# The MLP of a hybrid transformer block: residual parked in the output rows, five tiles for split weights, splits made three items ahead

## The chip, the cores and the metric

The kernel runs on one core of one Trainium2 chip. The metric is the device time of one execution in microseconds (us). A core has a matrix engine (TensorE, in the profile PE, with its weight loads shown apart as PEld), a vector engine (DVE), a scalar engine for activations (ACT), GpSimd (POOL) and SyncE (SP), which here only starts transfers. Transfers (DMAs) can be started from SP, ACT or POOL.

## What is computed

One layer of a sequence model on 256 tokens of width 2048, in float32. Three mixers (two kinds of attention and an RWKV-7 recurrence) read one normed projection and are mixed through gates and an output projection. The part that matters here comes after that:

```
x = x + rms_norm(mix, norm_mix_post)              # the residual: x1 in the kernel
hdn = square(relu(rms_norm(x, norm_mlp_pre) @ w_mlp_up))     # 2048 -> 8192
x = x + rms_norm(hdn @ w_mlp_down, norm_mlp_post)            # 8192 -> 2048, the output
```

The residual x1 is used three times: as input of the up projection, in a per-token mean of squares that corrects the last norm for the norm ahead of the MLP (which the kernel leaves out of the up projection), and as the summand of the output.

## The kernel before

**Split weights.** Each float32 weight tile of 128x1024 is loaded into a tile `raw` (L160-165; `raw2` for most weights of the down projection, L1326-1333). ACT rounds it to a high part (L173, tile `whi`), DVE subtracts to get the low part (L175, `wlo`), and TensorE multiplies with both. `wsplit` (L170) does this; `home[0]` may name other tiles for the result, otherwise it takes them from a ring of three `whi` and three `wlo`. Loads are started by SP, in the order of the program; a load waits until the tile that it overwrites is free.

**Residual.** x is loaded into two tiles `x1` of 128x2048 (one for each half of the tokens, 8 KB of each partition's memory, L1159), from a pool that lives to the end. `add_mixed` (L1170) adds the normed mixer output in place, in chunks of 512 columns; TensorE transposes the result (`turn`, L1192), and ACT and DVE turn that into the 16 packed tiles `upk2`. The engines' order is written out by hand up to L1279, for POOL too from L1238 on; behind it, a scheduler orders ACT, DVE, PE, POOL and the queues by their place in the program and by what is ready.

**The MLP's work list.** The up projection gives 64 column blocks of 128; a block is two items (halves of the contraction), each of 8 products of width 512 with the high part and 8 of width 256 with the low part (`up` L1370, `gemm` L187). The second half of a block ends with a product of its own line, L197. Then `hidden` (L1348) evacuates the PSUM bank: ACT copies half of it (L1351), DVE adds the other half (L1352), ACT does relu (L1353) and square (L1357) into a tile `pk`. In blocks 2 to 9 it also squares one chunk of x1 on ACT, summing it (L1361), and after eight of them DVE makes the per-token correction `eps4` (L1363-1368). The down projection of the first 14 of 16 row groups uses a Strassen-like scheme: 28 rounds `d`, each of seven items `F1` to `F7` of six products (L1434-1436), whose weights are sums of quarter tiles. The sums are made by DVE (L1411) and by accumulating transfers that POOL starts (L1414). Three or four up items stand between the seven items of a round: three in the eight rounds of the tuple `THREE`, four in the others. Three of four PSUM tiles `gps` hold F3, F7 and F1; the fourth serves the up items.

`drive` (L1301) walks over this list. For each item it first makes the split weights of the item itself and of the next AHEAD = 1 (L1309: the `prep` of `up` or `down`), then issues the products, and behind them the postponed work of the item before (`posts`: evacuations, and `forms`, which makes the combinations of the hidden activations; `sums`: the additions of the Strassen products).

**Memory.** Ahead of the MLP the pool `op` holds gains and weight tiles `kw`; it is closed at L1477, and in its room the pool `p3` is opened for the down projection (`fm`, `sfm`, `raw2`).

**Last stage** (L1563-1590). The last two row groups go through plain products with tokens on the output side (`tok`, L208), four groups of 512 columns with four weight tiles each. After each step `tick` takes one function from the list `hooks`, which holds three empty ones and then the remaining `sums`. For each group DVE adds the sums (L1578) and ACT squares (L1579). The second last group computes the norm's constant with `eps4` (L1584), the last one the factor (`rstd_of`, with a power on POOL, L1152), multiplies, adds x1 (L1588) and writes the output in ten transfers (L1589).

Of the kernel before, what the change touches and what calls it, by code (L numbers as in the profile page):

```python
# [19 lines left out]
D = 2048  # L20
KT = 16
AHEAD = 1
SHARE = 0.88
HALF = 1024
EPS = 1e-6
# [27 lines left out]
def hybrid_block(ctx, tc, xt, x, gains, params, consts, lora, gup, wst, out):  # L53
    nc = tc.nc
    V, A, G, PE = nc.vector, nc.scalar, nc.gpsimd, nc.tensor

    cpool = ctx.enter_context(tc.tile_pool(name="cpool", bufs=1))
# [8 lines left out]
    def nm(s):  # L66
        uid[0] += 1
        return f"{s}_{uid[0]}"
# [45 lines left out]
    each, hooks = [], []  # L114
# [43 lines left out]
    rawdma = [None]  # L158
# [8 lines left out]
    home = [None]  # L167
# [114 lines left out]
    def g1(w=T):  # L282
        return rp.tile([128, T], F32, tag="g1", name=nm("g1"), bufs=21)
# [83 lines left out]
    w = {(u, 0): [wpool.tile([128, HALF], F32R, tag=t, name=nm(t), bufs=3) for t in ("whi", "wlo")] for u in range(3)}  # L367
# [666 lines left out]
    for br in ("sb", "fox"):  # L1034
        for s in ("q", "k"):
# [3 lines left out]
            for h in range(4):  # L1039
                ps = unit(upk)  # L1040
                t = g1()
# [114 lines left out]
    for f in now:  # L1156
        f()
    loads = []
    x1 = [p2.tile([128, D], F32, tag="x1", name=nm("x1"), bufs=2) for _ in range(2)]  # L1159
    for c in range(0, D, 512):  # L1160
        for tt in range(2):
            loads.append(lambda tt=tt, c=c: nc.sync.dma_start(out=x1[tt][:, c:c + 512],
                                                              in_=x[tt * 128:tt * 128 + 128, c:c + 512]))
# [3 lines left out]
    def junk():  # L1167
        return p2.tile([128, 512], F32, tag="junk", name=nm("junk"), bufs=2)

    def add_mixed(tt, c, w):  # L1170
        V.scalar_tensor_tensor(x1[tt][:, c:c + w], mg[tt][:, c:c + w], r2[tt], x1[tt][:, c:c + w], ALU.mult, ALU.add)

# [90 lines left out]
    for b in range(4):  # L1263
        add_mixed(1, 512 * b, 512)
        turn(1, b)
# [14 lines left out]
    ss3 = cpool.tile([128, 2, 4], F32, name="ss3")  # L1280
# [18 lines left out]
    work, posts, sums, hl = [], [], [], {}  # L1299

    def drive():  # L1301


        while work:
            prep, run, quota = work.pop(0)
            if prep is None:
                run(None)
                continue
            for w in [(prep, run, quota)] + [w for w in work if w[0]][:AHEAD]:  # L1309
                if w not in hl:  # L1310
# [30 lines left out]
    eps4, sum4 = [], []  # L1341
    ss4 = cpool.tile([128, 2, 4], F32, name="ss4")
    ys = []
    hid, fmh, fml = {}, {}, {}

    squares = [(tt, c) for c in range(4) for tt in range(2)]

    def hidden(j, ps):  # L1348

        b, t = tmp(), tmp()  # L1350
        A.activation(b, ps[:, T:2 * T], AF.Copy)  # L1351
        V.tensor_tensor(t, ps[:, 0:T], b, ALU.add)  # L1352
        A.activation(t, t, AF.Relu)  # L1353
        if j % 2 == 0:
            hid[j // 2] = pk().bitcast(F32).rearrange("p (s t) -> p s t", s=4)
        h = hid[j // 2]
        last = A.activation(h[:, 0:4:3] if j % 2 == 0 else h[:, 1:3], t.rearrange("p (s t) -> p s t", s=2), AF.Square)  # L1357
        if j >= 2 and squares:
            tt, c = squares.pop(0)
            with tc.issue_after(last.ins):  # L1360
                A.activation(junk(), x1[tt][:, 512 * c:512 * c + 512], AF.Square, accum_out=ss3[:, tt, c:c + 1])  # L1361
        if j in (10, 11):
            e = cpool.tile([128, 2], F32, name=nm("eps4"))  # L1363
            V.tensor_reduce(e[:, 0:1], ss3[:, j % 2, :], AX.X, ALU.add)
            V.tensor_scalar(e[:, 0:1], e[:, 0:1], 1.0 / D, EPS, ALU.mult, ALU.add)
            V.tensor_tensor(e[:, 1:2], e[:, 0:1], e[:, 0:1], ALU.mult)
            V.tensor_scalar(e[:, 1:2], e[:, 1:2], EPS, None, ALU.mult)
            eps4.append(e[:, 1:2])

    def up(j):  # L1370

# [104 lines left out]

    po.close()  # L1477
    p3 = ctx.enter_context(tc.tile_pool(name="p3", bufs=1))

    def fm():  # L1480
        return p3.tile([128, 7, 128], F32R, tag="fm", name=nm("fm"), bufs=16)
# [25 lines left out]
    for j in range(2):  # L1507
        hidden(j, gp[j])
# [27 lines left out]
    last, count, free = [], 0, 0  # L1536
    first = [sum(SIZES[:q]) for q in range(len(SIZES) + 1)]
# [3 lines left out]
    for q in range(len(SIZES)):  # L1541
        for sb in range(2):
            for d, F in enumerate(down(q, sb)):
# [10 lines left out]
                last, count, free = [F[4]], count + 1, sb  # L1554
# [3 lines left out]
    while made[0] < 32:  # L1558
        work.extend(form())
    drive()  # L1560
    hooks.extend([lambda: None] * 3 + sums)

    hp = [hp[k] for k in range(4 * LAST, 64)]  # L1563
    g4, loads = gain(1, [pk() for _ in range(4)])
    side.extend(loads)

    def spare(n):

        if n < wst.shape[0] - 3:
            return None  # L1570
        return [p3.tile([128, HALF], F32, tag="raw2", name=nm("kw"), bufs=6).bitcast(F32R) for _ in range(2)]

    home[0] = spare
    for g in range(4):
        gs = slice(512 * g, 512 * g + 512)
        for tt, ps in enumerate(tok(hp, 4 if g == 3 else 1)):
            yv = ys[tt][:, gs]
            V.tensor_tensor(yv, yv, ps, ALU.add)  # L1578
            A.activation(junk(), yv, AF.Square, accum_out=ss4[:, tt, g:g + 1])  # L1579
            if g == 3:  # L1580
                r4 = rstd_of(ss4[:, tt, :], None, sum4[tt])
            V.tensor_tensor(yv, yv, g4[g], ALU.mult)
            if g == 2:
                sum4.append(rstd_of(ss4[:, tt, :], eps4[tt], None))  # L1584
            if g == 3:
                for c, w in (0, 512), (512, 512), (1024, 512), (1536, 256), (1792, 256):
                    cs = slice(c, c + w)
                    V.scalar_tensor_tensor(x1[tt][:, cs], ys[tt][:, cs], r4, x1[tt][:, cs], ALU.mult, ALU.add)  # L1588
                    (nc.scalar if c == 512 or w == 256 and c == 1536 else nc.sync).dma_start(  # L1589
                        out=out[tt * 128:tt * 128 + 128, cs], in_=x1[tt][:, cs])  # L1590


# [123 lines left out]
```

## Time and profile before

| | us |
|---|---|
| median of three runs | 1502.87 (1501.86 to 1506.22) |
| the profiled execution | 1503.08 |
| its span, first to last instruction | 1501.2 |
| PE busy | 1487.4 (99%) |
| DVE busy | 1205.8 (80%) |
| ACT busy | 933.3 (62%) |
| POOL busy | 94.7 (6%) |

The profile shows one execution. For each engine it has the busy time and the number of instructions, for groups of instructions the time of one and the idle time of the engine ahead of them with what ended it, and it can follow the chain of work that ended last back from the end. A busy PE is not a PE at its peak: a product is shown with a modelled end, and the next begins before that end. The MLP's items run from 829.1 us to 1447.95 us of the span, the last stage from there to the end.

### The profile page before, as it was taken

To read this page: it belongs to the slowest core of one execution; us is meant where nothing else is said; L and a number is where in the kernel's file an instruction comes from. 1 tells how busy PE (TensorE), PEld (TensorE's weight loads), DVE (VectorE), ACT (ScalarE), POOL (GpSimd) and SP (SyncE) were. 2 spreads that over 40 slices of the span, in tenths; PEclk is the share of its full clock that TensorE was granted. 3 is DMA by queue.
4 is the path that set the end of the run, shared out by engine and by line. 5 is a ranking of instruction groups with operands and counts; after the bars stand their busy time and mean duration, and the time that the engine had idled before them with its cause. 6 is when DMAs were issued, how large, how long until landed. Compare 5 with 4: busy or idle time off the path is not lost.

```text
span 1501.2 us, 22710 instructions
## 1 busy us (share of the span) xinstructions
PE 1487.4 (99%) x8384; PEld 1250.2 (83%) x8384; DVE 1205.8 (80%) x1677; ACT 933.3 (62%) x1431; POOL 94.7 (6%) x151
## 2 busy tenths in 40 slices
PE   9999999999999999999999999999999999999997
PEld 8888888887788887788888888888888888888886
DVE  7965779895687895476557688998999989999996
ACT  7665677555765445564545676776666666767663
POOL 0011003000002000000000000000000000000000
PEclk9999999999999999999999999999999999999999
DMA  8655445454555455455774868889898888989874
GB/s 288 202 154 175 154 161 172 152 182 154 164 174 174 156 183 183 131 174 191 243 235 153 267 181 256 250 223 260 259 257 256 229 268 250 262 259 262 255 218 148
DMA packets 107055, 312.19 MB, mean 208 GB/s; under 512 B 12352, under 2 KB 14400, under 8 KB 106944
## 3 DMA queue, kind: packets, MB, share of 16 engines
q1 hardware_dynamic: 96336, 279.35, 57.0%
q0 software_dynamic: 8064, 29.36, 10.3%
q10 hardware_dynamic: 2544, 2.03, 0.5%
q8 instruction: 66, 1.08, 0.3%
q14 instruction: 45, 0.37, 0.1%
HBM read 279.24 MB, written 2.10 MB: 187 GB/s over the span
## 4 chain that ended last, share of the span: by engine, by line
PE 96%; DMA 1%; DVE 1%; issue 1%; ACT 1%; SPq 0%; POOLq 0%; DVEq 0%; POOL 0%; ACTq 0%
PE gps L235 28%; PE gps L191 22%; PE gps L195 12%; PE gps L220 7%; PE mps L1434 3%; PE mps L1436 3%; PE mps L1435 3%; PE gps L1436 2%; PE gps L1434 2%; PE gps L1435 2%; PE gps L197 2%; PE gps L359 1%; DMA raw<-raw 1%; PE mps L840 1%; DMA raw<-in_wst_dram 1%
## 5 line engine op out<-in xcount | busy, mean ns | idle before, releaser
L175 DVE TENSOR_TENSOR wlo<-raw,whi 128x1024 fp32r<-128x1024 f32 x570 | 691.3, 1223 | 151.0 <-ACT whi L173 140.6
L173 ACT ACTIVATE whi<-raw 128x1024 fp32r<-128x1024 f32 x570 | 597.6, 1057 | 253.7 <-PE gps L235 71.8
L191 PE MATMUL gps<-pk,whi 128*128 128x512 f32 x1460 | 370.6, 392 | 0.5 <-DVE tmp L1352 0.2
L191 PEld LDWEIGHTS gps<-pk,whi 128*128 128x128 f32 x1460 | 270.4, 188 | 56.2 <-DVE tmp L1352 1.2
L235 PE MATMUL gps<-whi,pk 128*128 128x512 f32 x1004 | 253.5, 392 | 0.0
L195 PEld LDWEIGHTS gps<-pk,wlo 128*128 128x128 f32 x1561 | 212.7, 190 | 15.2 <-DVE wlo L175 0.3
L235 PEld LDWEIGHTS gps<-whi,pk 128*128 128x128 f32 x1004 | 186.5, 188 | 40.1 <-issue 1.0
L195 PE MATMUL gps<-pk,wlo 128*128 128x256 f32 x1561 | 218.0, 282 | 0.0
L235 PE MATMUL gps<-wlo,pk 128*128 128x512 f32 x502 | 138.2, 392 | 0.0
L235 PEld LDWEIGHTS gps<-wlo,pk 128*128 128x128 f32 x502 | 93.2, 188 | 19.6 <-issue 0.2
L1434 PE MATMUL mps<-whi,fm 128*128 128x512 f32 x224 | 88.6, 396 | 1.8 <-ACT whi L173 1.7
L1351 ACT ACTIVATE tmp<-gps 128x256 f32<-128x256 f32 x64 | 24.6, 385 | 102.8 <-PE gps L197 100.9
L1435 PE MATMUL mps<-whi,fm 128*128 128x512 f32 x224 | 87.7, 392 | 0.0
L1436 PE MATMUL mps<-wlo,fm 128*128 128x512 f32 x224 | 87.4, 390 | 0.0
L1414 POOL DMA_DIRECT2D raw<-raw x56 | 48.8, 872 | 572.7 <-DVE raw L1411 299.1
L1411 DVE TENSOR_TENSOR raw<-raw,raw 128x1024 f32<-128x1024 f32 x56 | 68.3, 1220 | 0.8
L1434 PE MATMUL gps<-whi,fm 128*128 128x512 f32 x168 | 65.8, 392 | 0.0
L1436 PE MATMUL gps<-wlo,fm 128*128 128x512 f32 x168 | 65.7, 391 | 0.0
L1435 PE MATMUL gps<-whi,fm 128*128 128x512 f32 x168 | 65.5, 390 | 0.0
L220 PE MATMUL gps<-whi,pk 128*128 128x512 f32 x224 | 60.7, 393 | 0.0
L1434 PEld LDWEIGHTS mps<-whi,fm 128*128 128x128 f32 x224 | 42.4, 189 | 10.0 <-ACT whi L173 3.9
L1436 PEld LDWEIGHTS mps<-wlo,fm 128*128 128x128 f32 x224 | 42.1, 188 | 9.4
(359 smaller groups left out, 1738.3 us busy)
## 6 DMA issues: line engine op xcount, KB each, us to landing
raw<-in_wst_dram SPq DMA_DIRECT2D x510, 512.0 KB, 4.4
raw<-raw POOLq DMA_DIRECT2D x56, 512.0 KB, 8.5
x<-in_xt_dram SPq DMA_DIRECT2D x8, 256.0 KB, 5.3
x<-in_x_dram SPq DMA_DIRECT2D x8, 256.0 KB, 5.3
raw<-in_wst_dram SPq DMA_DIRECT2D x6, 256.0 KB, 5.0
pk<-in_wst_dram SPq DMA_DIRECT2D x6, 256.0 KB, 5.2
g<-in_gains_dram SPq DMA_DIRECT2D x4, 256.0 KB, 4.8
pk<-in_gains_dram SPq DMA_DIRECT2D x4, 256.0 KB, 6.7
```

Of the source, the lines that this page charges most:

```text
L173: A.activation(hi, raw, AF.Copy)
L175: low = lambda: V.tensor_tensor(lo, raw, hi.bitcast(F32), ALU.subtract)
L191: PE.matmul(ps, hi[:, i * 128:i * 128 + 128], pks[i], start=first and i == 0, stop=False)
L195: PE.matmul(ps[:, 0:T], lo[:, i * 128:i * 128 + 128], pks[i][:, 0:T], start=False, stop=False)
L197: PE.matmul(ps, hi[:, (n - 1) * 128:n * 128], pks[n - 1], start=False, stop=True)
L220: PE.matmul(ps[tt], pks[k][:, c:c + 128], w[:, (k - k0) * 512:(k - k0) * 512 + 512], start=k == 0 and part == 0 and w is hl[0], stop=w is ...
L235: PE.matmul(ps[tt], pks[k][:, c:c + 128], w[:, (k - k0) * 512:(k - k0) * 512 + 512], start=k == 0 and part == 0 and w is hl[0], stop=False)
L1411: V.tensor_tensor(R[d, a], R[d, a], R[d, b], ALU.add)
L1414: G.dma_start(out=R[d, a], in_=R[d, b], accum_op=ALU.add)
L1434: PE.matmul(Q[f], a, w, start=d == d0 and i == 0, stop=False)
L1435: PE.matmul(Q[f], b, w, start=False, stop=False)
L1436: PE.matmul(Q[f], a, wl, start=False, stop=d == dn and i == 1)
```

## The change

1. `x1` comes from the pool `op`, which is closed before the down projection, so 16 KB of each partition come free. `add_mixed` writes each finished chunk into the rows of the output (8 transfers of 256 KB started by POOL).
2. In that room the pool `p3` gets two more pairs of tiles (`mhi`, `mlo`) for split weights. While `drive` runs, the splits go in turn to `mhi`, `whi`, `mhi`, `whi`, `whi`: a ring of five pairs.
3. `drive` makes the split weights of the next three items instead of the next one.
4. The squares of x1 and `eps4` leave `hidden`. In the last stage the eight chunks are read back from the output rows into `pk` tiles (8 transfers started by POOL, two with each of the first four hooks). From the tenth hook on, or behind the last of the sums if those reach further, one hook for each chunk squares it on ACT; the fourth chunk of each half is followed by the five small DVE operations of `eps4`.
5. The output is formed in the read-back tiles and written from there.

```
-    x1 = [p2.tile([128, D], F32, tag="x1", name=nm("x1"), bufs=2) for _ in range(2)]
+    x1 = [op.tile([128, D], F32, tag="x1", name=nm("x1"), bufs=2) for _ in range(2)]
...
     def add_mixed(tt, c, w):
         V.scalar_tensor_tensor(x1[tt][:, c:c + w], mg[tt][:, c:c + w], r2[tt], x1[tt][:, c:c + w], ALU.mult, ALU.add)
+        G.dma_start(out=out[128 * tt:128 * tt + 128, c:c + w], in_=x1[tt][:, c:c + w])
...
-            for w in [(prep, run, quota)] + [w for w in work if w[0]][:AHEAD]:
+            for w in [(prep, run, quota)] + [w for w in work if w[0]][:3]:
...
-        last = A.activation(h[:, 0:4:3] if j % 2 == 0 else h[:, 1:3], t.rearrange("p (s t) -> p s t", s=2), AF.Square)
-        if j >= 2 and squares:
-            tt, c = squares.pop(0)
-            with tc.issue_after(last.ins):
-                A.activation(junk(), x1[tt][:, 512 * c:512 * c + 512], AF.Square, accum_out=ss3[:, tt, c:c + 1])
-        if j in (10, 11):
...
+        A.activation(h[:, 0:4:3] if j % 2 == 0 else h[:, 1:3], t.rearrange("p (s t) -> p s t", s=2), AF.Square)
...
     p3 = ctx.enter_context(tc.tile_pool(name="p3", bufs=1))
+    turns = itertools.cycle((True, False, True, False, False))
+
+    def five(n):
+        if not next(turns):
+            return None
+        return [p3.tile([128, HALF], F32R, tag=t, name=nm(t), bufs=2) for t in ("mhi", "mlo")]
+
+    home[0] = five
...
+    def back(tt, c):
+        x1b[tt, c] = pk().bitcast(F32)
+        with tc.issue_after(rawdma[0].ins):
+            G.dma_start(out=x1b[tt, c], in_=out[128 * tt:128 * tt + 128, 512 * c:512 * c + 512])
+
+    def moment(tt, c):
+        A.activation(junk(), x1b[tt, c], AF.Square, accum_out=ss3[:, tt, c:c + 1])
+        if c == 3:
...
+    own = [(tt, c) for tt in range(2) for c in range(4)]
+    first = hooks[:]
+    hooks[:] = [lambda i=i: [back(*k) for k in own[2 * i:2 * i + 2]] + ([first[i]()] if i < len(first) else [])
+                for i in range(4)] + first[4:]
+    hooks.extend([lambda: None] * (9 - len(hooks)))
+    hooks.extend(lambda k=k: moment(*k) for k in own)
...
-                    V.scalar_tensor_tensor(x1[tt][:, cs], ys[tt][:, cs], r4, x1[tt][:, cs], ALU.mult, ALU.add)
+                    o = x1b[tt, c // 512][:, c % 512:c % 512 + w]
+                    V.scalar_tensor_tensor(o, ys[tt][:, cs], r4, o, ALU.mult, ALU.add)
```

More of the change, by code (lines that the diff above doesn't have):

```diff
@@ L1344, in hybrid_block @@
     hid, fmh, fml = {}, {}, {}
-    squares = [(tt, c) for c in range(4) for tt in range(2)]
     def hidden(j, ps):
@@ L1356, in hidden @@
         h = hid[j // 2]
-        last = A.activation(h[:, 0:4:3] if j % 2 == 0 else h[:, 1:3], t.rearrange("p (s t) -> p s t", s=2), AF.Square)
-        if j >= 2 and squares:
-            tt, c = squares.pop(0)
-            with tc.issue_after(last.ins):
-                A.activation(junk(), x1[tt][:, 512 * c:512 * c + 512], AF.Square, accum_out=ss3[:, tt, c:c + 1])
-        if j in (10, 11):
[L1363 to L1368, printed above, removed]
+        A.activation(h[:, 0:4:3] if j % 2 == 0 else h[:, 1:3], t.rearrange("p (s t) -> p s t", s=2), AF.Square)
     def up(j):
@@ L1565, in hybrid_block @@
     side.extend(loads)
+    x1b = {}
+    def back(tt, c):
[5 more added lines that the diff above has]
+        if c == 3:
+            e = cpool.tile([128, 2], F32, name=nm("eps4"))
+            V.tensor_reduce(e[:, 0:1], ss3[:, tt, :], AX.X, ALU.add)
+            V.tensor_scalar(e[:, 0:1], e[:, 0:1], 1.0 / D, EPS, ALU.mult, ALU.add)
+            V.tensor_tensor(e[:, 1:2], e[:, 0:1], e[:, 0:1], ALU.mult)
+            V.tensor_scalar(e[:, 1:2], e[:, 1:2], EPS, None, ALU.mult)
+            eps4.append(e[:, 1:2])
+    own = [(tt, c) for tt in range(2) for c in range(4)]
[4 more added lines that the diff above has]
+    hooks.extend(lambda k=k: moment(*k) for k in own)
     def spare(n):
@@ L1587, in hybrid_block @@
                     cs = slice(c, c + w)
-                    V.scalar_tensor_tensor(x1[tt][:, cs], ys[tt][:, cs], r4, x1[tt][:, cs], ALU.mult, ALU.add)
+                    o = x1b[tt, c // 512][:, c % 512:c % 512 + w]
+                    V.scalar_tensor_tensor(o, ys[tt][:, cs], r4, o, ALU.mult, ALU.add)
                     (nc.scalar if c == 512 or w == 256 and c == 1536 else nc.sync).dma_start(
-                        out=out[tt * 128:tt * 128 + 128, cs], in_=x1[tt][:, cs])
+                        out=out[tt * 128:tt * 128 + 128, cs], in_=o)
 def _cols(w, c0, n=128):
```

## The prediction

> **What bounds the kernel now.** I read the page's head first, then the chain that ended last, then the MLP stretch: its groups and its waits.
>
> ```profile
> PE 1487.4 (99%) x8384; PEld 1250.2 (83%) x8384; DVE 1205.8 (80%) x1677; ACT 933.3 (62%) x1431; POOL 94.7 (6%) x151
> PE 96%; DMA 1%; DVE 1%; issue 1%; ACT 1%; SPq 0%; POOLq 0%; DVEq 0%; POOL 0%; ACTq 0%
> ```
>
> TensorE is the bound, in busy time and in the chain. So the change can win only what TensorE loses between its products, and only in the MLP, where items are now prepared earlier. I work out that loss from the pace. The first row below is a piece of the chain, the next three are of the timeline, the last three are groups between 830 and 1448 us.
>
> ```profile
> 1447.95 8.16 PE gps L235 x36
> 829.11 2.00 PE L191 MATMUL gps<-pk,whi 128*128 128x512 f32 x8
> 1044.24 1.12 PE L195 MATMUL gps<-pk,wlo 128*128 128x256 f32 x8
> 1045.19 0.40 PE L1434 MATMUL mps<-whi,fm 128*128 128x512 f32 x1
> L195 PE MATMUL gps<-pk,wlo 128*128 128x256 f32 x992 | 138.3, 282 | 0.0
> L1434 PE MATMUL mps<-whi,fm 128*128 128x512 f32 x224 | 88.6, 396 | 1.8 <-ACT whi L173 1.7
> L1434 PE MATMUL gps<-whi,fm 128*128 128x512 f32 x168 | 65.8, 392 | 0.0
> ```
>
> A wide product takes 8.16/36 = 0.2267 us, a narrow one (1045.19-1044.24)/8 = 0.119. The up items have 992 narrow products and as many wide ones; the down items have 3 x (224+168) = 1176 wide. That makes 2168 x 0.2267 + 992 x 0.119 = 609.5 us. The stretch takes 1447.95-829.11 = 618.8, so 9.3 us lie above the pace. How much of it is waiting, the waits of the weight loads between 829 and 1500 us show:
>
> ```profile
> PEld mps L1434 <- ACT whi L173: 3.9, 5, 1.5
> PEld gps L191 <- DVE tmp L1352: 1.2, 2, 0.7
> PEld gps L191 <- ACT whi L173: 0.9, 2, 0.6
> PEld gps L1436 <- DVE wlo L175: 0.7, 2, 0.4
> PEld gps L1434 <- ACT whi L173: 0.5, 1, 0.5
> ```
>
> Five rows, 7.2 us, 12 waits. A weight load may start while the product ahead still runs, so each wait costs TensorE about 0.15 us less: 7.2 - 12 x 0.15 = 5.4 us. The other 3.9 us are 2 ns on each wide product and belong to no wait. Of the 5.4 us, late weights have 6.0 - 10 x 0.15 = **4.5 us**, a PSUM bank evacuated late 1.2 - 2 x 0.15 = 0.9. This is the whole stake: 0.36% of the time.
>
> **The change part by part. Three items ahead, ring of five.** With a ring of three and one item ahead, the split of item k+1 writes the tile of item k-2; with five and three, the split of k+3 writes the tile of k-2. So ACT is released at the same moment as before, with two more items, at least 2 x 1.36 = 2.7 us (six products each), lying ready. Does ACT ever get there? These rows, again of the MLP, say for what it waits:
>
> ```profile
> ACT tmp L1351 <- PE gps L197: 100.9, 61, 2.5
> ACT whi L173 <- PE mps L1435: 29.2, 36, 1.4
> ACT whi L173 <- DMA raw<-in_wst_dram: 10.1, 5, 3.6
> ```
>
> Mostly for TensorE, 10.1 us for weight transfers. ACT is ahead nearly always and is stopped by the ring, so the lead will build up. The longest single wait for weights is 1.5 us, below 2.7. I count all 4.5 us of late weights as gone and the 0.9 of late evacuation as staying. **-4.5 us** (bounds 0 and -5.4).
>
> **Write of x1.** Eight POOL issues, priced by the row of POOL's other issues:
>
> ```profile
> L1414 POOL DMA_DIRECT2D raw<-raw x56 | 48.8, 872 | 572.7 <-DVE raw L1411 299.1 <-DVE wlo L175 197.7 <-DMA raw<-in_wst_dram 56.4
> 815.71 0.56 POOL L1152 TENSOR_TENSOR rs<-rs,cst 128x1 f32<-128x1 f32 x1 [8.91 <-ACT rs L1151]
> 808.29 2.73 DVE L1171 SCALAR_TENSOR_TENSOR x<-mg,rs,x 128x512 f32<-128x512 f32 x4
> 817.95 2.73 DVE L1171 SCALAR_TENSOR_TENSOR x<-mg,rs,x 128x512 f32<-128x512 f32 x4
> raw<-raw POOLq DMA_DIRECT2D x56, 512.0 KB, 8.5
> ```
>
> The first four follow the additions that end by 811.02, so POOL is through by about 812.5; the power that the second half waits for comes at 815.71, 3 us later: hidden. The second four end by about 822.3, and POOL is next needed by the first L1414, in the down projection. Their data land some 8.5 us on (the median of the landing row, of transfers twice as large), by 831. That matters, because the first `mhi` may lie in the room of x1: its split (1.06 us, next fence) then ends by 832, and the third item, which needs it, starts two items of 8 x 0.2267 + 8 x 0.119 = 2.77 us behind 829.11, at 834.6. **0 us**; without that cover, what a landing of over 11 us would overrun.
>
> **Squares moved.** They leave blocks 2 to 9, where nothing waits for them (0 us), and join the last stage.
>
> ```profile
> L1361 ACT ACTIVATE junk<-x 128x512 f32<-128x512 f32 x8 | 4.9, 616 | 0.0
> L1361 ACT ACTIVATION_READ_ACCUMULATOR junk<-x 128x1 f32 x8 | 1.5, 187 | 0.0
> 1445.00:1450.00 5.00, 5.00 (x27) 4.32 (x26) 5.00 (x8) 3.33 (x6) 0.00 (x0) 1.00 0.48 157
> 1450.00:1455.00 5.00, 5.00 (x23) 4.14 (x23) 4.95 (x8) 2.22 (x3) 0.00 (x0) 1.00 0.68 203
> 1455.00:1460.00 5.00, 5.00 (x23) 4.13 (x23) 3.89 (x5) 2.29 (x4) 0.00 (x0) 1.00 0.76 243
> 1460.00:1465.00 5.00, 5.00 (x23) 4.13 (x22) 3.63 (x5) 3.06 (x5) 0.00 (x0) 1.00 0.57 197
> 1450.35 1.06 ACT L173 ACTIVATE whi<-raw 128x1024 fp32r<-128x1024 f32 x1 [0.26 <-DMA raw<-in_wst_dram]
> 1453.62 1.06 ACT L173 ACTIVATE whi<-raw 128x1024 fp32r<-128x1024 f32 x1 [2.21 <-DMA raw<-in_wst_dram]
> DMA to landing us min/median/max: 3.3/4.3/5.9
> ```
>
> TensorE takes 8.16/3 = 2.72 us for each weight tile here, so the third is needed at 1453.39 and the fourth at 1456.11; their high parts are ready at 1451.41 and 1454.68, **2.0 and 1.4 us** ahead. The moments need 4.9 + 1.5 = 6.4 us of ACT from about 1457 on, and between 1455 and 1465 ACT has 10 - 2.29 - 3.06 = 4.65 idle. The 1.75 us over slip into the next slice, or push splits back. Against that stands the lead brought from the MLP. I take 0.3 (bounds 0 and 1.75). The ten small operations of the corrections lie in DVE's idle time (10 - 3.89 - 3.63 in those slices).
>
> **Read-back.** 2.1 MB. At the rate of the fullest row (243 GB/s) that is 8.6 us of transfers; the four rows leave (0.52+0.32+0.24+0.43) x 5 = 7.6 us of idle transfer time. It fits, barely, and beside it a weight load will take longer than the 4.3 us (median) of the last row, that of the weight loads between 1438 and 1480 us. The crowded MLP gives the upper end:
>
> ```profile
> raw<-in_wst_dram SPq DMA_DIRECT2D x235, 512.0 KB, 6.4
> ```
>
> That is 2.1 us more; less the 1.4 us of lead, 0.7 us reach TensorE. Bounds: 0 (the lead of 2.7 us from the MLP covers it) and 8.5 - 4.3 = 4.2 (the other landing row above). I take **+0.7**. By the Trainium skill, "DMA: Bandwidth & Descriptors", section "Issuing engines are not separate DMA queues", starting transfers on several engines saves only issue time, since all run on the same 16 DMA engines and interleave; by that rule POOL's own queue shields no weight load; the term would be nearer 4.2 and the sum 1503.1.
>
> The read-back tiles hold the output at the end, so L1588 and the output transfers keep their number, size and order: 0.
>
> Sum: -4.5 + 0.3 + 0.7 = -3.5. Against the profiled execution's 1503.08: **1499.6**. The median of the runs shown is 1502.87, so this is -0.22% of it. About 0.3% (4.5 us) is what a measurement of this kernel can tell from no change; the forecast lies inside.
>
> **The rivals. (a) The lead doesn't come about**, because the weights themselves can't come earlier: the splits are three ahead in the program only.
>
> ```profile
> SPq L1331 <- DMA raw<-raw: 310.6, 54, 9.3
> ```
>
> For it: SP stops 54 times for an accumulating transfer, and all later loads queue behind. Against it: ACT waits 10.1 us for weight transfers in the whole MLP (above). Time: 1503.08 + 1.0 (the two costs above) = 1504.1.
>
> **(b) The evacuation queues behind the splits: slower.** The late evacuation shows how, in the chain:
>
> ```profile
> 1091.10 10.11 DMA raw<-raw
> 1101.82 8.44 DMA raw<-in_wst_dram
> 1110.36 1.07 ACT whi L173
> 1112.60 0.43 DVE tmp L1352
> 1113.07 2.14 PE gps L191 x8
> ```
>
> A late load held a split, the split held DVE's L1352, and that held the only PSUM bank of the up items. With three items ahead, up to two more subtractions can stand ahead of L1352 (their row below, 1.22 us each). The place is the end of a round, where a block's end and the next block's begin are parted by one down item: 1.36 us, of which evacuating takes about 0.86 (DVE's 0.43, and ACT's copy reckoned as long), leaving 0.5. One subtraction more costs 1.22 - 0.5 = 0.7 us, two 1.9. It decides from where DVE has less than that slack, as in this slice of the rounds with three up items:
>
> ```profile
> L175 DVE TENSOR_TENSOR wlo<-raw,whi 128x1024 fp32r<-128x1024 f32 x570 | 691.3, 1223 | 151.0 <-ACT whi L173 140.6
> 1300.00:1350.00 50.00, 49.96 (x252) 42.23 (x251) 49.35 (x59) 35.28 (x47) 4.34 (x5) 1.00 0.93 270
> ```
>
> Eight such rounds at 0.7 to 1.9, mean 1.3, are 10.4 us, and half the gain is lost: 1503.08 + 1.0 - 2.2 + 10.4 = **1512.3** (1507.5 with one subtraction each). Against it: over the whole, DVE waits for ACT (L175 <- L173, 140.6 us), and then the split of k+3 starts when item k-2 ends, as that of k+1 does now. The Trainium skill, "Perfetto Trace Analysis", section "Tensor Engine Instruction (MATMUL, LD_WEIGHTS)", says ACT, DVE and GpSimd are strict first-in-first-out; by it nothing overtakes a waiting split, which speaks for (b). The chain above agrees, once, with 1.2 us in two waits.
>
> **(c) The last stage starves**: read-back at its upper end, 4.2 us, and the squares at theirs: 1503.08 - 4.5 + 1.75 + 4.2 = 1504.5.
>
> **How the numbers follow.** Forecast 0.52, (a) 0.18, (b) 0.18, (c) 0.12. The forecast alone spans 1497.7 (5.4 gone, nothing added) to 1501.5; below 1498.36, where faster by over 0.3% begins, lies rather less than half of it: 0.22. Above 1507.4 lies (b): 0.18. The rest, 0.60, is within 0.3%. The range takes in the forecast, (a) and (c), 1497.3 to 1507.5, and leaves out (b), whose mild end it touches.
>
> **What would show it.** Right: weight loads wait for `whi` under 1 us in all, not 5.3 (first and third row of that fence and the last); ACT waits more for weight transfers; the MLP takes some 614 us, not 618.8. (a): those waits stay. (b): waits for L1352 grow from two to eight or more, most behind 1250 us. (c): waits of L235 for `whi`, of which there are none now. Wrong altogether: a gain over 5.4 us, or a loss ahead of 829 us.

## The result and the profile after

The changed kernel takes 1500.81 us (median of 22 runs, 1499.11 to 1503.08), the kernel before, in the same series, 1504.03 (1501.86 to 1507.43). The ratio on record is 0.9981, with a 95% interval of 0.9975 to 0.9987 (the two medians alone give 0.9979): a gain of 0.19% where 0.22% was forecast, clear of zero and inside the 0.3% that were called no change. The profiled execution of after took 1500.17 us, its span is 1498.4, 2.8 us shorter than the 1501.2 of before.

The page of after has the same head as that of before: TensorE is the bound, and the chain still lies on it.

```profile
PE 1485.5 (99%) x8384; PEld 1250.5 (83%) x8384; DVE 1204.3 (80%) x1677; ACT 932.3 (62%) x1431; POOL 102.9 (7%) x167
PE 95%; DMA 2%; DVE 1%; issue 1%; ACT 1%; DVEq 0%; POOLq 0%; POOL 0%; SPq 0%; ACTq 0%
```

The waits of the weight loads between 829 and 1500 us (engine, tile and line, what was waited for, then microseconds in all, times, longest):

```profile
PEld gps L191 <- DVE tmp L1351: 1.9, 7, 0.8
PEld gps L220 <- ACT whi L173: 0.7, 1, 0.7
PEld gps L220 <- DVE wlo L175: 0.5, 1, 0.5
```

Lines have moved: the evacuation on DVE is L1351 now (L1352 before), the products of the down items are L1422 to L1424 (L1434 to L1436), DVE's sum of weights L1399 (L1411), the squares of x1 L1570, the splits still L173 and L175. The four kinds of wait for `whi` and `wlo` in the work list are gone, 6.0 us in ten waits; the wait for a late evacuation has grown from 1.2 us in two to 1.9 in seven; two waits of the last stage (L220) are new.

Three points of TensorE's timeline show where the 2.8 us come from. The first fence is the kernel before (its first product at 829.11 stands in the prediction), the second is after: first product of the work list, first of the last stage, and the last 18 products.

```profile
1447.79 1.98 PE L235 MATMUL gps<-whi,fm 128*128 128x512 f32 x8
1487.23 4.24 PE L220 MATMUL gps<-kw,fm 128*128 128x512 f32 x18
```

```profile
829.36 2.00 PE L191 MATMUL gps<-pk,whi 128*128 128x512 f32 x8
1443.70 1.98 PE L235 MATMUL gps<-whi,fm 128*128 128x512 f32 x8
1484.00 4.24 PE L220 MATMUL gps<-kw,fm 128*128 128x512 f32 x18
```

| us | before | after | difference |
|---|---|---|---|
| start of the work list | 829.11 | 829.36 | +0.25 |
| work list, to the first L235 | 618.68 | 614.34 | -4.34 |
| last stage, to its last 18 products | 39.44 | 40.30 | +0.86 |
| from there to the end | 13.97 | 14.40 | +0.43 |
| span | 1501.2 | 1498.4 | -2.80 |

The work list gave what was expected, and 1.3 us of it go again behind it. How 0.86 of them go in the last stage, the chain of this stretch, ACT and PE show:

```profile
1435.63 10.40 DMA raw<-in_wst_dram
1446.12 1.07 ACT whi L173
...
1448.47 4.03 DMA raw<-in_wst_dram
1452.60 1.07 ACT whi L173
```

```profile
1458.36 0.62 ACT L1570 ACTIVATE junk<-pk 128x512 f32<-128x512 f32 x1
...
1461.42 0.62 ACT L1570 ACTIVATE junk<-pk 128x512 f32<-128x512 f32 x1
...
1462.04 2.95 ACT L173 ACTIVATE whi<-raw 128x1024 fp32r<-128x1024 f32 x3
```

```profile
1463.13 1.19 PE L220 MATMUL gps<-whi,fm 128*128 128x512 f32 x4 [0.23 <-ACT whi L173]
```

Six squares of x1 stand in a row on ACT, 3.7 us of them, and three splits start only behind the last; the product at 1463.13 waits for the first of these. The row itself comes behind a split at 1452.60, and that one behind two weight loads, one behind the other, of which the first took 10.40 us. The read-back ran beside that first load and had landed by 1447.3 us. These are the rows of the two new transfers (median us from issue to landing last), and POOL's:

```profile
out_dram<-x POOLq DMA_DIRECT2D x8, 256.0 KB, 3.8
pk<-out_dram POOLq DMA_DIRECT2D x8, 256.0 KB, 10.2
```

```profile
1430.09 3.57 POOL L1567 DMA_DIRECT2D pk<-out_dram  x6
1436.42 1.07 POOL L1567 DMA_DIRECT2D pk<-out_dram  x2 [2.77 <-PE gps L195]
```

The prediction set the read-back into the last stage. POOL issued it 7 to 14 us ahead of that: six transfers as soon as its last accumulating transfer was out, two more when a product of the up items (L195) had released them.

### The profile page after: what moved, and what is told of

The parts are those of the page before. It is cut to its first block, busy times and chain, and to the rows that moved or that the text cites. A ratio compares the mean times of both kernels' runs of the same rounds, so it can differ in the third digit from the quotient of the medians.

```text
span 1498.4 us, 22705 instructions
## 1 busy us (share of the span) xinstructions
PE 1485.5 (99%) x8384; PEld 1250.5 (83%) x8384; DVE 1204.3 (80%) x1677; ACT 932.3 (62%) x1431; POOL 102.9 (7%) x167
## 4 chain that ended last, share of the span: by engine, by line
PE 95%; DMA 2%; DVE 1%; issue 1%; ACT 1%; DVEq 0%; POOLq 0%; POOL 0%; SPq 0%; ACTq 0%
PE gps L235 26%; PE gps L191 23%; PE gps L195 13%; PE gps L220 6%; PE mps L1422 3%; PE mps L1423 3%; PE mps L1424 3%; PE gps L1422 3%; PE gps L1423 3%; PE gps L1424 3%; DMA raw<-in_wst_dram 2%; PE gps L197 2%; PE gps L359 1%; PE mps L840 1%; PE gps L1224 1%
## 5 line engine op out<-in xcount | busy, mean ns | idle before, releaser
L175 DVE TENSOR_TENSOR wlo<-raw,whi 128x1024 fp32r<-128x1024 f32 x442 | 539.3, 1225 | 133.1 <-ACT whi L173 122.0
L173 ACT ACTIVATE whi<-raw 128x1024 fp32r<-128x1024 f32 x442 | 464.9, 1057 | 208.0 <-PE gps L235 69.5
L191 PE MATMUL gps<-pk,whi 128*128 128x512 f32 x1114 | 283.2, 393 | 0.4 <-DVE tmp L1351 0.4
L235 PE MATMUL gps<-whi,pk 128*128 128x512 f32 x1004 | 253.5, 392 | 0.0
L191 PEld LDWEIGHTS gps<-pk,whi 128*128 128x128 f32 x1114 | 205.7, 188 | 42.2 <-DVE tmp L1351 1.3
L235 PEld LDWEIGHTS gps<-whi,pk 128*128 128x128 f32 x1004 | 186.5, 188 | 40.1 <-issue 1.0
L195 PEld LDWEIGHTS gps<-pk,wlo 128*128 128x128 f32 x1193 | 162.6, 190 | 11.6 <-DVE wlo L175 0.3
L175 DVE TENSOR_TENSOR mlo<-raw,mhi 128x1024 fp32r<-128x1024 f32 x128 | 156.4, 1222 | 16.6 <-ACT mhi L173 15.4
L195 PE MATMUL gps<-pk,wlo 128*128 128x256 f32 x1193 | 166.7, 282 | 0.0
L173 ACT ACTIVATE mhi<-raw 128x1024 fp32r<-128x1024 f32 x128 | 135.3, 1057 | 42.8 <-PE mps L1423 10.5
L235 PE MATMUL gps<-wlo,pk 128*128 128x512 f32 x502 | 138.2, 392 | 0.0
L235 PEld LDWEIGHTS gps<-wlo,pk 128*128 128x128 f32 x502 | 93.2, 188 | 19.5 <-issue 0.2
L191 PE MATMUL gps<-pk,mhi 128*128 128x512 f32 x346 | 86.4, 390 | 0.0
L1350 ACT ACTIVATE tmp<-gps 128x256 f32<-128x256 f32 x64 | 24.5, 382 | 93.6 <-PE gps L197 90.7
L191 PEld LDWEIGHTS gps<-pk,mhi 128*128 128x128 f32 x346 | 64.5, 188 | 13.8 <-DVE tmp L1351 0.6
L1399 DVE TENSOR_TENSOR raw<-raw,raw 128x1024 f32<-128x1024 f32 x56 | 68.5, 1222 | 0.8
L220 PE MATMUL gps<-whi,pk 128*128 128x512 f32 x224 | 60.7, 393 | 0.0
L195 PEld LDWEIGHTS gps<-pk,mlo 128*128 128x128 f32 x368 | 50.2, 190 | 3.6
L1422 PE MATMUL mps<-whi,fm 128*128 128x512 f32 x132 | 51.9, 393 | 0.0
L1423 PE MATMUL mps<-whi,fm 128*128 128x512 f32 x132 | 51.7, 392 | 0.0
L1424 PE MATMUL mps<-wlo,fm 128*128 128x512 f32 x132 | 51.5, 390 | 0.0
```

Of the source, the lines that this page charges most:

```text
L173: A.activation(hi, raw, AF.Copy)
L175: low = lambda: V.tensor_tensor(lo, raw, hi.bitcast(F32), ALU.subtract)
L191: PE.matmul(ps, hi[:, i * 128:i * 128 + 128], pks[i], start=first and i == 0, stop=False)
L195: PE.matmul(ps[:, 0:T], lo[:, i * 128:i * 128 + 128], pks[i][:, 0:T], start=False, stop=False)
L220: PE.matmul(ps[tt], pks[k][:, c:c + 128], w[:, (k - k0) * 512:(k - k0) * 512 + 512], start=k == 0 and part == 0 and w is hl[0], stop=w is ...
L235: PE.matmul(ps[tt], pks[k][:, c:c + 128], w[:, (k - k0) * 512:(k - k0) * 512 + 512], start=k == 0 and part == 0 and w is hl[0], stop=False)
```

## Theories and experiments

Main theory: late weights were the stake, the lead in a deeper ring takes them away, and what is lost again comes from the squares. Against it: the ring or the lead alone would do; evacuations late behind splits decide (the prediction's (b)); the read-back is the loss of the last stage (its (c)). Twelve kernels, each timed against the kernel before on the same chip. The stages are those of the table above, from one profiled execution each; those of ring-only (1506.43 us) and of after, fenced (1507.87) lie furthest from their medians.

| kernel | work list | last stage | median | ratio to before (95%) |
|---|---|---|---|---|
| ring of five only | 620.7 | 40.9 | 1504.07 | 1.0009 (1.0000-1.0018) |
| three ahead only | 637.2 | 41.1 | 1523.54 | 1.0140 (1.0127-1.0153) |
| residual's traffic only | 619.5 | 41.4 | 1506.34 | 1.0024 (1.0015-1.0034) |
| squares spread | 615.4 | 39.5 | 1500.05 | 0.9982 (0.9973-0.9991) |
| ring only, fenced | 633.3 | 43.8 | 1522.29 | 1.0128 (1.0113-1.0144) |
| read back twice | 614.5 | 48.5 | 1507.44 | 1.0031 (1.0020-1.0042) |
| after, fenced | 618.1 | 43.6 | 1510.13 | 1.0046 (1.0033-1.0059) |
| after, fenced, spread | 618.1 | 41.1 | 1506.63 | 1.0031 (1.0019-1.0044) |
| two ahead | 616.3 | 39.6 | 1501.04 | 0.9988 (0.9979-0.9997) |
| four ahead | 615.2 | 40.3 | 1500.85 | 0.9981 (0.9972-0.9989) |
| ring only, wider gap | 615.7 | 39.9 | 1502.05 | 1.0000 (0.9989-1.0011) |
| spread, wider gap | 615.0 | 39.4 | 1500.56 | 0.9984 (0.9975-0.9992) |

**Ring of five only.** After, with the lead of before:

```
-            for w in [(prep, run, quota)] + [w for w in work if w[0]][:3]:
+            for w in [(prep, run, quota)] + [w for w in work if w[0]][:AHEAD]:
```

> The ring of five stays, the program makes splits one item ahead again; the rest of the change is kept. Main theory (a lead needs both: the room, and the splits standing early in the program): the MLP, 614.3 us with the change and 618.7 before, goes most of the way back, 617 to 618.5, and weight loads wait for whi or mhi again, 4 us or more; the run is 3 to 4 us slower than with the change, within 1 us of the kernel before. Rival A (the ring alone does it, since ACT runs on as soon as tile and data are there, whatever the place in the program): MLP 614 to 615, no waits for weights. The last stage (39.4 us before, 40.3 after) stays at 40.3 by both, as the squares stay in it.

The weight waits of the work list are gone here too (0.2 us left), and yet the gain isn't there: its place is taken by evacuations.

```profile
PEld gps L191 <- DVE tmp L1351: 6.8, 7, 2.6
```

The largest, on DVE and then on PE:

```profile
1372.73 1.23 DVE L175 TENSOR_TENSOR wlo<-raw,whi 128x1024 fp32r<-128x1024 f32 x1 [2.40 <-ACT whi L173]
1373.87 1.22 DVE L175 TENSOR_TENSOR mlo<-raw,mhi 128x1024 fp32r<-128x1024 f32 x1
1375.12 1.23 DVE L1399 TENSOR_TENSOR raw<-raw,raw 128x1024 f32<-128x1024 f32 x1
1376.26 0.42 DVE L1351 TENSOR_TENSOR tmp<-gps,tmp 128x256 f32<-128x256 f32 x1
```

```profile
1376.74 3.65 PE L191 MATMUL gps<-pk,whi 128*128 128x512 f32 x8 [2.18 <-DVE tmp L1351]
```

This is the mechanism of (b), in full: ACT had waited 4.05 us for an accumulating transfer, DVE idled 2.40 for ACT, and then two subtractions and a sum stood ahead of the evacuation. Counted in the order that the scheduler built, two splits stand ahead of each evacuation on DVE in the kernel before; here it is four at 51 of 62, in after four at 60. So the number of splits ahead doesn't tell ring-only and after apart.

**Three ahead only.** After, with the ring of three (`home[0] = five` left out).

> Splits three items ahead in the program, but in the ring of three as before. Main theory: the split of item k+3 needs the tile of item k, so no lead beyond that of before can come about; MLP 618 to 620 us, weight waits as before (some 5 us), 1 to 2 us slower than the kernel before because the last stage's loss stays. Rival B (what counts is the place in the program: a split that stands ahead of an evacuation and must wait for its tile holds the evacuation back): waits for DVE's addition of the evacuation (7 with the change) grow to 20 or more, MLP 625 us and over. Rival A (only readiness counts): as the main theory.

The worst of the series: the size that rival B named, but not by its way. The first rows are waits of weight loads, the last one is ACT's:

```profile
PEld gps L1422 <- ACT whi L173: 15.1, 18, 0.9
PEld mps L1422 <- ACT whi L173: 6.2, 18, 1.7
...
PEld gps L191 <- DVE tmp L1351: 2.1, 11, 0.2
```

```profile
ACT whi L173 <- PE gps L197: 91.3, 50, 2.2
```

In after ACT's wait for the end of an up block (L197) is booked to the evacuation, `tmp L1350`; here the split of item k+3 stands ahead of it and waits for the tile of item k itself. Nearly all of the loss is late weights; late evacuations cost 2.1 us of waits, in eleven and not in twenty or more.

**The residual's traffic without ring and lead** (one item ahead, ring of three, everything else as in after).

> Only the way of the residual over the output rows, with the squares in the last stage; ring of three, one item ahead. Main theory (the squares, eight in the last stage, cost what the last stage lost): MLP 618 to 619 us, last stage 40 us or more (39.4 before), in sum 1 to 2 us slower than the kernel before; this is the price of the room. Rival C (the lead from the MLP covers the last stage): without that lead the last stage loses more than with the change, 41 us or more. Rival D (the loss in the last stage is chance): last stage 39.4 to 39.6.

The price of the room: 0.8 us in the work list, 2.0 in the last stage, where one product waits for a split, 1.7 us at the weight load:

```profile
PEld gps L220 <- ACT whi L173: 1.7, 1, 1.7
```

The lead halves that (0.86 in after), as the prediction's step on the squares had it (one execution each).

**Squares spread.** After each square one hook stays empty:

```
-    hooks.extend(lambda k=k: moment(*k) for k in own)
+    for k in own:
+        hooks.extend([lambda k=k: moment(*k), lambda: None])
```

> The change with one empty hook behind each square, so that the eight squares stand at every second hook instead of at each. Main theory (with the change seven squares run one behind the other on ACT, 1458.4 to 1462.0 us, ahead of a split that is then late; the data of that split had landed): last stage 39.4 to 39.6 us instead of 40.3, no wait of L220 for whi, 0.9 to 1.3 us faster than with the change, as far as a time can tell. Rival E (the read-back's transfers are the cause, not ACT): last stage stays at 40.0 or more.

The last stage is back at 39.50 us and the tail at 14.0, with the same read-back:

```profile
1444.69 1.98 PE L235 MATMUL gps<-whi,fm 128*128 128x512 f32 x8
...
1484.19 4.24 PE L220 MATMUL gps<-kw,fm 128*128 128x512 f32 x18
```

So without the row the loss is gone, though the weight loads beside the read-back were as slow here (three of 9.46 to 10.64 us, worked out from the trace) as in after (9.21 to 10.40; in the kernel before, three loads at this place took 3.75 to 6.79). The time can't be told from after's; in the profiled execution one late evacuation of 1.3 us in the work list takes the gain back, and what did so in the others no profile shows.

The row alone isn't the cause either. In after and six kernels of the table (ring of five only, three ahead only, residual's traffic only, two ahead, four ahead, and ring only with the wider gap) three splits follow the row of six. The last 18 products begin 21.96 to 21.98 us behind the first of these splits in six of the seven (22.25 in three ahead only), so that split sets the length of the stage. Counted from the stage's first product it starts 18.34 us on in after, but 17.57 with two ahead, and there the same row costs 0.1 us. In all seven it stands 9.4 to 9.7 us behind the fourth split of the stage, which in all but three ahead only waits for a weight load. So a late load and the row behind it make the loss together, one after the other. That the read-back made the load late was not shown: in the spread kernel with the wider gap, four loads beside the read-back took only 4.44 to 7.15 us.

**Ring only, fenced.** While the work list runs, each split is issued behind the evacuation that stands ahead of it in the program, on ACT and DVE:

```
...
+        if gate_:
+            with tc.issue_after(gate_[0].ins):
+                A.activation(hi, raw, AF.Copy)
+            with tc.issue_after(gate_[1].ins):
+                V.tensor_tensor(lo, raw, hi.bitcast(F32), ALU.subtract)
+            wq.append((hi, lo))
+            return
...
+        gate_[:] = [A.activation(b, ps[:, T:2 * T], AF.Copy), V.tensor_tensor(t, ps[:, 0:T], b, ALU.add)]
...
```

> The ring of five without the lead in the program (as in the ring-only kernel, 1504.07 us), but while the work list runs each split is issued behind the latest evacuation of an up block that stands ahead of it in the program, on ACT and on DVE: two splits instead of four then stand ahead of each evacuation. Theory of the order (the ring-only kernel lost because late splits stood ahead of evacuations): waits for evacuations fall from its 6.8 us to under 2, the MLP from 620.7 to 614-616, the time to 1499.5-1501.5. Rival 1 (its loss came from elsewhere, transfers or clock): the MLP stays above 619, the time about 1504. Rival 2 (a split that waits behind an evacuation comes too late, as in the kernel with three ahead in a ring of three, though five tiles leave it some 2 us more): waits for weights of 5 us or more, 1505 or later.

The theory of the order fell. Two splits instead of four stand ahead of each evacuation, and the waits for evacuations are 8.7 us at the weight loads, not under 2, beside some 13 us of waits for weights. The chain of this stretch, and DVE, show how (in this kernel the split's subtraction is L178, the sum L1406, the evacuation L1358):

```profile
1213.02 10.03 DMA raw<-in_wst_dram
```

```profile
1224.22 1.23 DVE L178 TENSOR_TENSOR wlo<-raw,whi 128x1024 fp32r<-128x1024 f32 x1 [3.84 <-ACT whi L176]
1225.37 1.22 DVE L1406 TENSOR_TENSOR raw<-raw,raw 128x1024 f32<-128x1024 f32 x1
1226.50 0.42 DVE L1358 TENSOR_TENSOR tmp<-gps,tmp 128x256 f32<-128x256 f32 x1
```

A load of 10.03 us holds ACT and DVE, and with them the evacuation, as in ring-only. ACT waits 43.6 us for transfers in the work list here, 15.9 in after. Why the loads come later was not shown. Late splits that free their raw tiles late aren't it by SP's waits: it waits less for splits here than in ring-only (183 us, 223 there) and more for accumulating transfers (294, 241).

**Read back twice** (the transfer of `back` issued a second time, into the same tile).

> After, with each chunk of the residual read back twice into the same tile (4.2 MB instead of 2.1; the second transfer waits for the first, so the squares move back too). If the read-back's traffic reaches TensorE, as the prediction's 0.7 us has it, the last stage grows by 0.7 us or more, up to 4.2, to 41.0 us and more until its last 18 products, and the weight loads between 1435 and 1460 us take longer. If the squares alone were the loss, the last stage stays within 0.4 us of the 40.3 of after, or gains up to 0.8 since the squares come later; time 1500-1501.

Neither: the last stage grows by 8.2 us. Two rows of ACT first, then one of the chain, then one of PE:

```profile
1445.40 0.63 ACT L1571 ACTIVATE junk<-pk 128x512 f32<-128x512 f32 x1 [5.51 <-DMA pk<-out_dram]
...
1460.89 1.06 ACT L173 ACTIVATE whi<-raw 128x1024 fp32r<-128x1024 f32 x1 [5.64 <-DMA raw<-in_wst_dram]
```

```profile
1452.22 8.57 DMA raw<-in_wst_dram
```

```profile
1462.00 2.11 PE L235 MATMUL gps<-whi,fm 128*128 128x512 f32 x8 [2.09 <-ACT whi L173]
```

The first square waits 5.5 us for its chunk and holds all splits behind it; so raw tiles come free late, a load issued at 1452.22 takes 8.57 us beside the second read-back, and TensorE waits most in three places, for 2.09, 1.15 and 2.22 us. The last of these comes behind six squares in a row again, so not all of the growth is the read-back's, and traffic and queue can't be parted in this run. What it shows is that a read-back of twice the size is no longer hidden. The Trainium skill, "DMA: Bandwidth & Descriptors", section "Issuing engines are not separate DMA queues", says that transfers started by different engines run on the same 16 DMA engines and interleave, so that POOL's own queue would shield no weight load; the landing of 8.57 us agrees.

**After, fenced**, with the evacuations emitted ahead of the splits, and the same **with the squares spread**.

> After, with each split issued behind the latest evacuation ahead of it in the program, and the evacuations emitted ahead of the splits: three splits instead of four stand ahead of each evacuation, and the splits still lie three items ahead. Theory of the order: waits for evacuations fall from 1.9 us in seven to about 1.0 in two or three, the MLP from 614.3 to 613.5 us, time 1499.5-1500.8, hardly to be told from after. Rival (a split that waits behind an evacuation is late): waits for weights come back, 1502 or more.

> The kernel before this one, with the squares of the last stage spread, one behind every second hook. Both theories of after's remaining loss together (evacuations behind splits 0.5-1 us, squares in a row 0.8 us in the last stage and 0.4 in the tail): MLP 613.5, last stage 39.5, tail 14.0: 1498.5-1499.5 us. If either is wrong, 1500 or more.

Both slower, as the rival of the first had it. The waits for evacuations fall to 1.4 us in one, but weights are late again, in the work list and in the last stage (L1434 is a down product of this kernel, L243 is in its last stage, L199 is its up product; all from after, fenced):

```profile
PEld gps L243 <- DVE wlo L178: 2.8, 1, 2.8
PEld gps L1434 <- ACT whi L176: 1.7, 1, 1.7
PEld gps L199 <- DVE tmp L1363: 1.4, 1, 1.4
```

Spreading the squares shortens the last stage here too, from 43.6 to 41.1 us.

**Two ahead, four ahead** (`[:2]` and `[:4]` in place of `[:3]`).

> After, with two items ahead in the program instead of three; ring of five, everything else as in after. In the built order four splits stand ahead of 55 of 62 evacuations on DVE and three ahead of seven (one ahead in the program: 51 and 11; three: 60 and 2). If the ring gives the lead and the program's lead only shifts where late sums and evacuations stand, the time lies between 1504.07 us (one) and 1500.81 (three), some 1502, with 2 to 6 us of waits for evacuations and none for weights. If the program's lead is what brings transfers forward, waits of ACT for transfers grow over after's 15.9 us in the work list, and the time is 1503 or more.

> After, with four items ahead instead of three. In the built order five splits instead of four stand ahead of 55 of 62 evacuations, and the fifth writes the tile of the very item whose evacuation it stands ahead of, as with three ahead in a ring of three (1523.54 us). If that is the rule (the lead in the program may be no more than the ring less two), every evacuation begins at least one split (1.06 us of ACT, 1.22 of DVE) later: the MLP grows by 10 us or more and the time is 1510-1525. If five tiles leave enough ready that a late evacuation alone does no harm, the time stays within 1500-1504.

Two ahead came out as expected, a little above after. Four ahead refutes the rule of its expectation, that the lead may be no more than the ring less two. Its weight loads, then ACT:

```profile
PEld gps L191 <- DVE tmp L1351: 6.3, 30, 0.3
```

```profile
ACT whi L173 <- PE gps L197: 53.7, 29, 2.9
ACT mhi L173 <- PE gps L197: 31.8, 18, 1.9
```

As with three ahead in a ring of three, a split stands ahead of most evacuations (47 of ACT's waits for the end of a block are a split's); worked out from the start times of the 62 evacuations, DVE's begins 2.43 us (median) behind the block's last product in both kernels, 0.69 in after. But here it costs 0.05 us each time and 1.8 in all. PE's order says why: the scheduler orders PE too, and where up blocks were six or seven products apart at 21 places in after, thirteen (2.97 us) stand between at most of them now. So an evacuation that is this late need not cost anything, and it isn't what cost 20 us in the ring of three; there the waits are for weights. That the shorter ring makes the weights late, the two kernels show together; by which step, they don't.

**Wider gap.** The item F4 goes ahead of the up item, which puts twelve products between blocks nearly everywhere; once on the ring-only kernel, once on the spread one.

```
-                work.extend([F[3], *some(1), *last])
+                work.extend([F[3], *last, *some(1)])
```

> The ring-only kernel (1504.07 us) with the order of the work list changed at one place: the item F4 of the round before goes ahead of the up item behind F3 instead of behind it. The built order then has twelve or more products (2.74 us) between the end of one up block and the start of the next at 52 of 55 places in the rounds; before, after and the ring-only kernel have only six to eight (1.38 us) at about 21 to 24 of them, and four ahead has them at 6. Theory: the late evacuations cost TensorE time only where that gap is narrow. The stalls of the ring-only kernel, 1.67, 0.98 and 2.34 us with 1.6 us of slowed clock behind the last, shrink by 1.36 each: waits for evacuations from 6.8 to about 2 us, the MLP from 620.7 to 615.5-616.5, the time to 1499-1501. Rival: the transfers hold everything back, whatever stands between: the MLP stays above 619, the time at 1503 or more.

> After with both remedies: the squares of the last stage spread as in the spread kernel (1500.05 us), and F4 ahead of the up item as in the kernel before this one. By the same theory the one stall of the spread kernel's work list (1.26 us) goes, the MLP takes 613.8-614.3 us, the last stage 39.5 to its last 18 products, the tail 14.0: 1498.0-1499.5 us, the best of the series. If the narrow gap is not what lets late evacuations reach TensorE: 1500 or more.

On ring-only the profiled execution does what was expected: waits for evacuations 3.4 us instead of 6.8, work list 615.7 instead of 620.7. The medians don't settle it: 1502.05 against 1504.07, with intervals that overlap. The single runs of both scatter widely, 1500.2 to 1508.0 and 1501.0 to 1507.3, so that one profile is a poor witness for either. On the spread kernel the gap gave nothing, and the forecast of 1498.0 to 1499.5 was missed. One late evacuation of 1.7 us remains, and it can't be the narrow gap, as twelve products stand there before and after the change:

```profile
1407.64 0.68 DVE L1429 TENSOR_TENSOR y<-y,junk 128x512 f32<-128x512 f32 x1
1408.24 1.22 DVE L1399 TENSOR_TENSOR raw<-raw,raw 128x1024 f32<-128x1024 f32 x1
1409.38 0.41 DVE L1351 TENSOR_TENSOR tmp<-gps,tmp 128x256 f32<-128x256 f32 x1
```

Here DVE is full: in the 19 us ahead of it, additions of products, sums of weights and splits follow one another with one pause of 0.61 us. No version of the series is measurably faster than after.

## Why the prediction was right, and where it was not

**The stake and -4.5 us: right.** Gaps over the pace of a product come to 5.42 us of TensorE in the work list before and 0.86 in after, a fall of 4.56; the stretch takes 614.34 us where some 614 was said. The waits for `whi` there went from 5.3 to nothing. ACT's waits for weight transfers grew only from 10.1 to 11.2, in these two rows between 829 and 1443 us (those for accumulating transfers from 2.5 to 4.7):

```profile
ACT whi L173 <- DMA raw<-in_wst_dram: 5.7, 5, 3.1
ACT mhi L173 <- DMA raw<-in_wst_dram: 5.5, 4, 1.8
```

**"The lead will build up": right, by a longer way.** The high part of an item was ready 2.7 us ahead of its first use before and 6.0 after (medians over the items, worked out from the trace). The ring alone does that too, since the scheduler moves splits forward as far as tiles are free. What the lead in the program adds is not settled: its sums and loads stand earlier in the built order (seven sums on DVE stand one evacuation later with the ring alone), and with two to four ahead the runs scatter less. That this order is the cause was only argued, and against it stands that with two ahead five of the sums stand later too, at no measurable cost.

**Write of x1, 0 us: right**, with a landing of 3.8 us instead of the 8.5 taken over. The 0.25 us at the start arise long before the MLP, most of them at 345.7 us.

**Squares, +0.3, and read-back, +0.7: the two terms are one, and each was reckoned wrongly.** Together they cost 0.86 us in the last stage, where 1.0 was said. The step that failed for the squares is that ACT has 4.65 us idle between 1455 and 1465: idle time summed over a stretch says nothing of an order in which six squares come together, with splits behind them. Their need was even overestimated: 6.4 us counts the activation and its reading one behind the other, but in the row above a square starts every 0.61 us, which is 4.9 for eight. (A half's correction is four small operations of 0.15 to 0.16 us, not five.) For the read-back the direction fits, as weight loads beside it took longer; but it ran beside the end of the work list, and the loads there took up to 10.40 us where 6.4, at most 8.5, was reckoned. How much of the 0.86 us is the read-back's, no run shows. That the two terms come out near the sum is in part luck.

**The rest of the loss was not forecast.** The 0.43 us at the end don't belong to the squares: nine kernels of the series that keep them together take 13.98 to 14.12 us from the last 18 products to the end, and one of the three that spread them 14.41. In after DVE comes to the last addition of products late, at 1483.22 behind other work, and waits 0.42 us for TensorE there in the spread kernel. With them the losses are +1.29 behind the work list, where +1.0 was forecast.

**Rivals.** (a) fell: the weights did come earlier. (b)'s mechanism is real, seven waits in after where its sign was eight or more, but they are 1.9 us in all: its price of 0.7 to 1.9 us a round held the order of TensorE fixed, and four ahead shows that order moving with it. (c) did not happen in after at its price of 4.2 and 1.75 us; with the read-back doubled, the waits of L235 for `whi` that it named are there, 4.9 us in three.

## What to carry to other kernels

A lead needs tiles for it: splitting further ahead in a ring that is too short cost 1.4%, the same lead in a ring of five gained 0.2%, the ring of five without the lead nothing, and leads of two to four can't be told apart there. Work that moves to a crowded stage should be spread in its engine's order, one piece at a time, whatever that engine's idle time sums to, and its price depends on how late the stage's first loads are. Before pricing a queue that grows on one engine, look at whether the scheduler that built it will also rearrange the engine that waits.

## What the runs showed of the hardware

The granted clock can fall after a short stop of TensorE. Ring-only, in stretches of 2 us around the stall that begins at 1374.4 (columns: busy time of PE, PEld, DVE, ACT, POOL, then granted clock, transfer share, GB/s); the last two lines are ring-only, fenced, after a stop of 2.26 us that ends at 1226.97:

```profile
1374.00:1376.00 2.00, 0.56 (x3) 0.14 (x1) 1.97 (x2) 0.86 (x1) 0.00 (x0) 1.00 0.91 213
1376.00:1378.00 2.00, 1.26 (x3) 1.07 (x4) 2.00 (x4) 1.51 (x3) 0.00 (x0) 0.67 0.99 326
1378.00:1380.00 2.00, 2.00 (x6) 1.52 (x6) 1.88 (x3) 0.69 (x2) 0.16 (x1) 0.50 0.83 310
1226.90:1229.00 2.10, 2.03 (x9) 1.68 (x10) 1.80 (x3) 2.05 (x4) 0.84 (x1) 1.00 1.02 409
1229.00:1231.00 2.00, 2.00 (x14) 1.82 (x13) 2.00 (x4) 1.94 (x3) 0.00 (x0) 1.00 0.95 293
```

A stop of 2.18 us was followed by some 3 us at half clock: of the eight products behind it six took 427 ns instead of 227 and two 595 and 334, in all 1.7 us more, on top of the stop. Three ahead only shows the same after 1.41 and 0.53 us of waiting close together (at 1464.54 and 1465.80). But neither the length nor the closeness decides: stops of 2.26 us (above), 2.34 (after, fenced, 1452.55) and 2.22 (read back twice, 1471.41) left the clock at 1.00, and so did waits of 1.42 and 0.52 close together (after, fenced, 887.53 and 888.78). What decides it, these runs don't show. The Trainium skill, "TensorE: Matmul & The Clock Gate", section "Why this matters for your kernels", warns of idle gaps over about 3 us; here shorter ones were sometimes enough.
